# A hybrid attention and gMLP block on one core: small constants loaded at the end of the u stage, later weights of the vs stage issued behind the last token tile, squares tied two tiles behind the casts

## The chip, the cores and the metric

The kernel runs on one core of one Trainium2 chip. The time is device time in microseconds (us), from the start of one execution to its end. Three runs of the kernel before gave 931.64, 933.08 and 933.76 us, a median of 933.08. A profiled execution gives, beside its time, a trace of every instruction on every engine: TensorE (PE in the profile), its weight loads (PEld), VectorE (DVE), ScalarE (ACT), GpSimd (POOL) and SyncE (SP), which issues most of the data transfers (DMAs).

## The reference

One layer on 1024 tokens of width 1024, in float32:

```python
h = rmsnorm(x, norm_g)
q, k, v, za, u, vs, zs, gm = split(h @ w_in)
a   = window_sink_attention(rope(q), rope(k), v, att_sinks)   # 16 heads, one sink per head
a   = (a * silu(za)) @ w_att_out
vn  = layernorm(gelu(vs), sg_ln_g, sg_ln_b)
sgo = gelu(u) * (mask(sg_w) mixed over blocks of 128 tokens with vn, + sg_b)
sgo = (sgo * silu(zs)) @ w_sg_out
ga, gs = sigmoid(gm + b_merge)
out = rmsnorm(x + (ga * a + gs * sgo) @ w_o, final_g)
```

The change touches the parts that make `vs` and `u`, and the loads of five small inputs: `att_sinks` (16 numbers), `b_merge` (2048), `sg_ln_g` and `sg_ln_b` (1024 each), and the mixing weights `sg_w` (eight matrices of 128 x 128).

## The kernel before

**How a product is made.** Each float32 operand is split into a high part, which the matmul's number format holds exactly, and a low part, the rest (`split`, L155 on ACT and L156 on DVE). A product of two operands is then three matmuls: high by high, high by low, low by high. On top of this a projection of 1024 x 1024 by 1024 x 1024 is cut into 2 x 2 quarters, and these are multiplied by seven products instead of eight. The tokens' sums and differences for this are called forms: b11, b21, t1, t2, t3, b22, t4. The weights' sums are called s1 to s4; a11, a12, a21, a22 are the weights' quarters themselves.

**The vs stage (0 to about 106 us).** It is written out step by step, since the forms are made here for the first time. For each of eight token tiles (128 tokens by 1024) `load_x` issues a load into one of three buffers named wr (L487), `scale_of` squares and sums it on ACT (L536, the square is written to a throw-away buffer) and makes the reciprocal root, and `turned_half` scales half a tile on DVE (L544), transposes its four 128 x 128 blocks on PE (L548) and leaves them in a PSUM bank. `form_of` casts a form's high part on ACT (L559) and takes the low part on DVE (L560). Tiles 0 to 3 go through `first_tile`, tiles 4 to 7 through `second_tile`, which also adds quarters on POOL by DMAs that accumulate (`add_on`, L531). Between the tiles stand the products that are possible so far: `first_product` (a11 and a12), `by_s1`, `by_s4`. Then follow, each over the two halves of the weights, the late products t2 by s2, t3 by s3 and t4 by a22 (`late_product`).

**Which loads this stage needs.** Beside x: a11, a12, s1 at the start; s3, which is a21 loaded into the place of s1 (`load_part`, L612, two DMAs) and then increased by a11 with two accumulating DMAs; a22 (two DMAs into wr buffers); and the mixing weights mix_w (L778, into the buffer wT, whose earlier tenant is the throw-away buffer of the squares). A quarter of mix_w is set to zero by a memset on DVE (L779). The small constants are `sink_sb` (L841, two loads, each 64 partitions of four runs of 8 bytes), its negative `nsink_sb` (L844, one DVE operation), `bm_sb` (L845), `lg_sb` (L846) and `lb_sb` (L847), the last two 128 partitions of 32 bytes each. nsink and sinks are read in the attention stage, lg and lb in the mixing of the u stage, bm near the end of the program.

**The u stage (about 106 to 240 us)** makes u by `gemm_pair` for four pairs of column blocks. A pair has the products b11, t1, t2, b21, t3, b22, t4, in this order. The first, t2's, t3's and t4's share one PSUM accumulator; it is copied or added to x11, x12, x22 as it grows, in L359, L366 (ACT) and L376 (DVE: x22 −= accumulator). The t4 matmuls of a pair write that accumulator again, so they wait for L376. Between products `split_next` loads and splits the weights of later pairs (wr, L200, two rows of weights per pair, then L155, L156 and the sums L242), and `hook` runs the mixing of finished blocks (`mix`: matmuls L890, then L898 and L906 on DVE, and a store L457).

**What sets the order.** The program is written in one order, but a planner sets each engine's order from the dependences and its own costs. So in SP's order of the kernel before, the two sink loads, bm, lg, lb and the first bias load (L876) stand among the loads of x tiles 5 and 6, though they are written behind the t4 product. Three helpers bind the order: `after(second, first)` ties two instructions of one engine in order, without a semaphore; `paced(move)` makes a DMA's issue wait for the instruction last put into `pace[0]`, a product's last matmul or an ACT copy; and the buffers themselves. Every engine, and SP's and POOL's DMA issuing, runs its own instructions strictly in order.

Of the kernel before, what the change touches and what calls it, by code (L numbers as in the profile page):

```python
# [30 lines left out]
P = 128  # L31
# [21 lines left out]
def hybrid_tile(  # L53
# [16 lines left out]
    nc = tc.nc  # L70
# [12 lines left out]
    def bank(tag, dt=F32):  # L83
        return psum.tile([P, 512], dt, name=nm("ps_" + tag), tag="ps_" + tag, bufs=2)

    def mtile(shape, dt, tag, bufs, pool=None):
        return (pool or main).tile(shape, dt, name=nm(tag), tag=tag, bufs=bufs)
# [4 lines left out]
    def raw_tile():  # L92
        return mtile([P, D], F32, "wr", 3)
# [9 lines left out]
    ident = const.tile([P, P], F32, name="ident")  # L103
# [6 lines left out]
    sink_sb = const.tile([P, 8], F32, name="sink_sb")  # L110
    nsink_sb = const.tile([P, 8], F32, name="nsink_sb")
    bm_sb = const.tile([P, 16], F32, name="bm_sb")
    lg_sb = const.tile([P, KC], F32, name="lg_sb")
    lb_sb = const.tile([P, KC], F32, name="lb_sb")
# [15 lines left out]
    def rstd_of(ss, scale, base=EPS, n=1):  # L130

        ve = mtile([P, n], F32, f"st{n}", 16 if n == 1 else 5)
        nc.vector.tensor_scalar(ve[:], ss, scale, base, op0=ALU.mult, op1=ALU.add)
        rt = mtile([P, n], F32, f"st{n}", 16 if n == 1 else 5)
        nc.scalar.activation(rt[:], ve[:], AF.Sqrt)
        r0 = mtile([P, n], F32, f"st{n}", 16 if n == 1 else 5)
        nc.vector.reciprocal(r0[:], rt[:])
        e = mtile([P, n], F32, f"st{n}", 16 if n == 1 else 5)
        if n == 1:
            nc.vector.scalar_tensor_tensor(e[:], ve[:], r0[:], r0[:], op0=ALU.mult, op1=ALU.mult)  # L140
        else:
            nc.vector.tensor_mul(e[:], ve[:], r0[:])
            nc.vector.tensor_mul(e[:], e[:], r0[:])
        nc.vector.tensor_scalar(e[:], e[:], -0.5, 1.5, op0=ALU.mult, op1=ALU.add)
        nc.vector.tensor_mul(e[:], e[:], r0[:])
        return e
# [11 lines left out]
    def after(second, first):  # L158

        tc.add_manual_dep(  # L160
            second.ins,
            first.ins.name,
            mybir.DependencyInfo(mybir.DependencyClass.NoSync, mybir.DependencyReason.DATA),
            reason="order",
        )
# [5 lines left out]
    def slot(name, shape=(P, 4, HALF), dt=F32R):  # L171

        return mtile(list(shape), dt, "T_" + name, 1)
# [28 lines left out]
    def begin_job():  # L202
        n = len(begun)
        if n < written[0]:
            begun.append(n)
            units.extend(jobs[n]())
# [25 lines left out]
    def half_of(half):  # L232
        return slice(half * HALF, (half + 1) * HALF)
# [44 lines left out]
    pace = [None]  # L278

    def paced(move):  # L280

        if pace[0] is not None:
            tc.add_manual_dep(
                move.ins,
                pace[0].ins.name,
                mybir.DependencyInfo(mybir.DependencyClass.Sync, mybir.DependencyReason.DATA),
                reason="pace",
            )
# [159 lines left out]
    def part_of_early(every=2):  # L448
        hooks[0] += 1
        if early and hooks[0] % every == 0:  # L450
            early.pop(0)()
# [33 lines left out]
    def load_x(t):  # L485
        xt = raw_tile()
        nc.sync.dma_start(xt[:], x[t * P : (t + 1) * P, :])  # L487
        return xt
# [32 lines left out]
    def raw_sum(t):  # L521
        return x_place(0, 1, t)

    def raw_b21(t):
        return x_place(1, 0, t)

    g_of = list(g_in)
    casts, lows = [], []

    def add_on(dst, src):  # L530
        nc.gpsimd.dma_start(dst, src, accum_op=ALU.add)  # L531

    def scale_of(t):
        xt = x_in[t] if t in x_in else load_x(t)
        ss = mtile([P, 1], F32, "st1", 16)
        square = nc.scalar.activation(junk[:], xt[:], AF.Square, accum_out=ss[:])  # L536
        if t == 1:

            after(square, casts[-1])
        return xt, rstd_of(ss[:], 1.0 / D)  # L540

    def turned_half(xt, r, j):
        cs = half_of(j)
        nc.vector.scalar_tensor_tensor(xt[:, cs], xt[:, cs], r[:], g_of[j], op0=ALU.mult, op1=ALU.mult)  # L544
        pt = bank("sc")
        for i in range(4):
            k = j * 4 + i
            nc.tensor.transpose(pt[:, i * P : (i + 1) * P], xt[:, k * P : (k + 1) * P], ident[:])  # L548
        return pt

    def form_of(name, t, src, minus=False):
# [28 lines left out]
    def second_tile(t):  # L580
        xt, r = scale_of(t)
        if t == 4:
            hb.update(new_b(("t1", "b22")))
            f22.append(slot("t4l", dt=F32))
        pt = turned_half(xt, r, 0)
        nc.vector.tensor_sub(raw_sum(t), raw_sum(t), pt[:])
        nc.scalar.mul(nf12[t - 4][:], pt[:], -1.0)
        form_of("t1", t, by_k(raw_sum(t)))
        pt = turned_half(xt, r, 1)
        form_of("b22", t, by_k(pt[:]))  # L590
        nc.scalar.copy(f22[0][:, t - 4, :], pt[:])
        add_on(nf12[t - 4][:], f22[0][:, t - 4, :])

    def raw_t2(t):
        nc.vector.tensor_add(raw_sum(t), raw_sum(t), f22[0][:, t - 4, :])
        add_on(raw_b21(t), raw_sum(t))

    def w_vs(i, j, c):
        return w[W_VS + 4 * i + 2 * j + c]

    def two_k(v, c):
        return v[:, 2 * c : 2 * c + 2, :]

    def flat(v):
        return v.rearrange("p k n -> p (k n)")

    raws = {}

    def load_part(name, at, i, j):
        raws[name] = slot(at, dt=F32)  # L610
        for c in range(2):
            nc.sync.dma_start(flat(two_k(raws[name], c)), w_vs(i, j, c))  # L612

    def load_vs(c):
        nc.sync.dma_start(flat(two_k(raws["a11" if c < 2 else "a12"], c % 2)), w[W_VS + c])
# [10 lines left out]
    def split_w(name, c, src=None, behind=False):  # L626
        hi, lo = pair_of_w()
        (split_behind if behind else split)(hi[:], lo[:], flat(two_k(raws[name], c)) if src is None else src)
        keep_w(name, c, hi, lo)
# [20 lines left out]
    def vs_product(acc, name, t, weight, fresh, last=True, cs=(0, 1)):  # L650
        bh, bl = hb[name]
        for c in cs:
            for n in range(3):
                for k in (2 * c, 2 * c + 1):
                    wh, wl = vs_w[weight, k]
                    lt = (bh, bh, bl)[n][:, k, tokens(t)]
                    rt = (wh, wl, wh)[n]
                    mm = nc.tensor.matmul(
                        acc[:],
                        lt,  # L660
                        rt,
                        start=fresh and k == 0 and n == 0,
                        stop=k == 3 and n == 2,
                        skip_group_check=True,
                    )
        return mm
# [14 lines left out]
    def by_s1(t):  # L681
        t5s[t] = bank("o" if t < 2 else "sc")
        vs_product(t5s[t], "t1", t, "s1", True)
        nc.scalar.mul(x_place(1, 1, t), t5s[t][:], -1.0)

    def by_s4(t):
        vs_product(t5s[t], "b22", t, "s4", False)
# [10 lines left out]
    x_in[1] = load_x(1)  # L698
    split_vs(1)
    second = scale_of(1)  # L700
    for c in (2, 3):
        load_vs(c)
# [34 lines left out]
    raw_t2(4)  # L737
    by_s1(0)
    by_s1(1)
    load_part("s3", "t4h", 1, 0)  # L740
    for c in range(2):
        add_on(flat(two_k(raws["s3"], c)), w_vs(0, 0, c))
    second_tile(7)
    for t in range(4):
        to_x11(t)
    for t in (5, 6, 7):
        raw_t2(t)
    by_s4(0)
    by_s4(1)
    a22 = []  # L750
    for c in range(2):
        a22.append(raw_tile())
        nc.sync.dma_start(a22[c][:], w_vs(1, 1, c))
    by_s1(2)
    by_s1(3)
    split_w("s2", 0, behind=True)
# [18 lines left out]
                statistics(t + i, 0)  # L775

    mix_w = mtile([P, KC, P], F32, "wT", 1, pool)
    nc.sync.dma_start(mix_w[:], sg_w)  # L778
    nc.vector.memset(mix_w[64:128, :, 0:64], 0.0)  # L779
    ones = mtile([P, P], F32R, "ones", 1, pool)  # L780
    nc.vector.tensor_scalar(ones[:], ident[:], 0.0, 1.0, op0=ALU.mult, op1=ALU.add)
# [52 lines left out]
            nc.tensor.matmul(row_sums[half][:], ones[:], part[:, half_of(half)], start=n == 0, stop=n == 1)  # L834
    split_w("a22", 1, a22[1][:])
    part_of_early(1)
    begin_job()
    late_product("t4", "a22", to_x21, [split_next, lambda: gelu_of(4, 1), lambda: gelu_of(6, 1)])
    of_head = sinks.rearrange("(c e r) -> e c r", e=2, r=2)
    for e in range(2):  # L840
        nc.sync.dma_start(  # L841
            sink_sb[e * 64 : (e + 1) * 64].rearrange("p (c r) -> p c r", r=2), of_head[e].partition_broadcast(64)
        )
    after(nc.vector.tensor_scalar_mul(nsink_sb[:], sink_sb[:], -1.0), lows[-1])  # L844
    nc.sync.dma_start(bm_sb[:], b_merge)  # L845
    nc.sync.dma_start(lg_sb[:], ln_g)  # L846
    nc.sync.dma_start(lb_sb[:], ln_b)  # L847
    for _ in range(2):
        split_next()

# [3 lines left out]
    late = []  # L854
# [68 lines left out]
        gemm_pair(hb, finish, both)  # L923
    while late:
        late.pop(0)()
    stage.close()


# [768 lines left out]
    for p in range(4):  # L1697
        n, t, acc, x11 = N_PAIRS + p, T_ORDER[p], accs[p], firsts[p]
# [173 lines left out]
```

## Time and profile before

| | |
|---|---|
| three runs | 931.64, 933.08, 933.76 us |
| the profiled execution, its own time | 930.13 us |
| span of its trace | 928.4 us |
| instructions | 13190 |
| mean granted TensorE clock | 0.992 |
| busy PE, DVE, ACT, POOL | 898.3, 697.0, 526.9, 141.5 us |

How to read the rows that follow. A row of a timeline has the start in us, the duration in us, the engine, the line of the kernel, the operation, what it writes <- what it reads, the shapes, how many equal instructions the row groups, and in brackets the idle time before it and the instruction that ended it. SPq is SP's queue, where a row is the issue of a DMA, not its transfer. A row of windows has the window, its length, busy time and count for PE, PEld, DVE, ACT and POOL, the granted clock of PE (1.00 is full speed), the mean busy share of the DMA engines and the GB/s moved. The landing of a load is not a row of its own; it is read from the instruction that waited for it.

### The profile page before, as it was taken

Reading aid. Unit: us, or ns where it says so; the run is one execution under the profiler, and the core shown is the slowest. Engines: PE = TensorE matmul, PEld = TensorE weight load, DVE = VectorE, ACT = ScalarE, POOL = GpSimd, SP = SyncE. Lnnn points to the kernel's source line nnn. Section 1 sums busy time; section 2 is a strip of 40 time slices with the busy share of each in tenths; the row PEclk is TensorE's granted clock in tenths of the full one; section 3 lists DMA queues with packets and bytes.
Section 4 is the critical chain, followed back from the end, with each engine's and each line's share of the span. In section 5 each row is a group of like instructions: output and inputs, shape, how many; then the busy total and the mean of one; then the engine's idle time right before and its main releaser. Section 6 shows DMA issues by size and latency. Waiting matters only on the chain.

```text
span 928.4 us, 13190 instructions
## 1 busy us (share of the span) xinstructions
PE 898.3 (97%) x4284; PEld 746.8 (80%) x4284; DVE 697.0 (75%) x1263; ACT 526.9 (57%) x1058; POOL 141.5 (15%) x204
## 2 busy tenths in 40 slices
PE   8879989999999999999999999999998999999996
PEld 6668868888888778888888888888886887888885
DVE  6768695666668667887878888747798589579986
ACT  7647433333454466786667677756575475458443
POOL 2121212223011001120111111101100110210012
PEclk9999989999999999999999999999999999999999
DMA  8894968895778776678787777989868755998632
GB/s 295 224 241 114 269 207 166 151 193 176 258 252 265 237 228 148 200 214 185 197 215 235 246 232 186 235 303 379 276 244 316 259 201 160 296 301 294 204 113 114
DMA packets 131598, 209.57 MB, mean 226 GB/s; under 512 B 12649, under 2 KB 61033, under 8 KB 131530
## 3 DMA queue, kind: packets, MB, share of 16 engines
q1 hardware_dynamic: 110072, 149.74, 48.0%
q0 software_dynamic: 21312, 58.73, 28.1%
q8 instruction: 34, 0.56, 0.2%
q14 instruction: 34, 0.28, 0.1%
q10 hardware_dynamic: 146, 0.27, 0.1%
HBM read 147.74 MB, written 86.11 MB: 252 GB/s over the span
## 4 chain that ended last, share of the span: by engine, by line
PE 74%; DMA 9%; DVE 9%; issue 4%; ACT 1%; POOL 1%; SPq 1%; DVEq 0%; POOLq 0%; ACTq 0%
PE ps_mm L341 35%; PE ps_o L341 25%; PE ps_sc L1202 3%; DMA wr<-in_w_dram 3%; DMA T_t4h<-in_w_dram 3%; PE ps_tp L341 3%; PE ps_o L1287 2%; PE ps_sc L341 2%; PE ps_tp L1246 2%; DMA T_t3h<-T_t4h 2%; DVE wl L156 2%; PE ps_tp L890 2%; DVE bq L185 1%; DMA sums<-in_w_dram 1%; DVE xh L868 1%
## 5 line engine op out<-in xcount | busy, mean ns | idle before, releaser
L155 ACT CAST wh<-s 128x1024 fp32r<-128x1024 f32 (+1 forms) x78 | 78.1, 1004 | 86.0 <-PE ps_mm L341 46.8
L156 DVE TENSOR_TENSOR wl<-wr,wh 128x1024 fp32r<-128x1024 f32 (+1 forms) x78 | 73.1, 940 | 43.6 <-ACT wh L155 43.1
L155 ACT CAST wh<-wr 128x1024 fp32r<-128x1024 f32 (+1 forms) x78 | 64.0, 824 | 60.3 <-PE ps_mm L341 31.7
L156 DVE TENSOR_TENSOR wl<-s,wh 128x1024 fp32r<-128x1024 f32 (+1 forms) x78 | 90.9, 1166 | 9.1 <-ACT wh L155 9.0
L341 PE MATMUL ps_o<-T_t1h,wh 128*128 128x512 f32 x148 | 58.8, 397 | 0.8 <-ACT wh L155 0.7
L341 PE MATMUL ps_o<-T_b22h,wh 128*128 128x512 f32 x148 | 58.2, 394 | 0.0
L341 PE MATMUL ps_o<-T_b22l,wh 128*128 128x512 f32 x148 | 57.9, 391 | 0.0
L341 PE MATMUL ps_o<-T_b22h,wl 128*128 128x512 f32 x148 | 57.8, 390 | 0.0
L341 PE MATMUL ps_o<-T_t1h,wl 128*128 128x512 f32 x148 | 57.7, 390 | 0.0
L341 PE MATMUL ps_o<-T_t1l,wh 128*128 128x512 f32 x148 | 57.6, 389 | 0.0
L341 PE MATMUL ps_mm<-T_b11h,wl 128*128 128x512 f32 x140 | 54.8, 392 | 2.9 <-DVE wl L156 2.9
L341 PE MATMUL ps_mm<-T_t3h,wh 128*128 128x512 f32 x140 | 55.5, 397 | 2.0 <-ACT x L366 2.0
L341 PE MATMUL ps_mm<-T_t4h,wh 128*128 128x512 f32 x140 | 55.2, 394 | 0.8 <-DVE x L376 0.7
L341 PE MATMUL ps_mm<-T_t3l,wh 128*128 128x512 f32 x140 | 55.3, 395 | 0.6 <-DVE T_t3l L156 0.6
L341 PE MATMUL ps_mm<-T_t3h,wl 128*128 128x512 f32 x140 | 55.4, 395 | 0.0
L341 PE MATMUL ps_mm<-T_b11h,wh 128*128 128x512 f32 x140 | 55.2, 395 | 0.0
L341 PE MATMUL ps_mm<-T_b11l,wh 128*128 128x512 f32 x140 | 54.8, 392 | 0.0
L341 PE MATMUL ps_mm<-T_t4h,wl 128*128 128x512 f32 x140 | 54.7, 391 | 0.0
L341 PE MATMUL ps_mm<-T_t2l,wh 128*128 128x512 f32 x140 | 54.6, 390 | 0.0
L1215 ACT ACTIVATE pr<-ps_sc,sm 128x192 f32<-128x192 f32 (+2 forms) x128 | 50.8, 408 | 6.7 <-DVE sm L1211 5.5
L341 PE MATMUL ps_mm<-T_t2h,wl 128*128 128x512 f32 x140 | 54.5, 390 | 0.0
L341 PE MATMUL ps_mm<-T_t4l,wh 128*128 128x512 f32 x140 | 54.5, 390 | 0.0
(384 smaller groups left out, 2404.1 us busy)
## 6 DMA issues: line engine op xcount, KB each, us to landing
wr<-in_w_dram SPq DMA_DIRECT2D x86, 256.0 KB
sums<-in_w_dram POOLq DMA_DIRECT2D x20, 512.0 KB, 7.9
s<-sums SPq DMA_DIRECT2D x20, 512.0 KB
q_hl<-qhl SPq DMA_DIRECT2D x16, 512.0 KB
q<-q_hl SPq DMA_DIRECT2D x64, 128.0 KB
y_dr<-x POOLq DMA_DIRECT2D x28, 256.0 KB, 6.5
wr<-in_w_dram SPq DMA_DIRECT2D x12, 512.0 KB
g<-in_w_dram POOLq DMA_DIRECT2D x12, 512.0 KB, 6.6
```

The lines of the kernel that those rows point to most:

```text
L155: nc.scalar.copy(hi, src)
L156: return nc.vector.tensor_sub(lo, src, hi.bitcast(F32))
L185: op(dst[:, i : i + 2, :], a[:, i : i + 2, :], c[:, i : i + 2, :])
L341: nc.tensor.matmul(acc, lt, rt, start=fresh and k == 0 and n == 0, stop=k == 3 and n == 2, skip_group_check=True,)
L868: nc.vector.tensor_scalar(xh[:, t, :], xh[:, t, :], mv[:, t, 0:1], r[:, t : t + 1], op0=ALU.subtract, op1=ALU.mult)
L890: nc.tensor.matmul(pm[:, t * P : (t + 1) * P], xh[:, half * 4 + t, g * P : (g + 1) * P], bias[-1][1][:, g % 4, :], start=True, stop=True,)
L1202: nc.tensor.matmul(sc[:, i, k0:], q_of[:, c, i * P : (i + 1) * P], kt[:, f, k0:], start=f == 0, stop=f == 1,)
L1215: nc.scalar.activation(held_in[c, i], sc[:, i, lo:hi], AF.Exp, bias=nmax[:, c, i : i + 1], scale=-1.0, accum_out=sums[:, c, i : i + 1],)
L1246: nc.tensor.transpose(dst, pr[:, i, block * P : block * P + width], ident[:])
L1287: nc.tensor.matmul(po[:, cs], lt, rt, start=n == 0, stop=n == len(terms) - 1)
```

## The change

Five things are edited. The loads of s3, of a22 and of mix_w get a dependence on the last transpose emitted so far, which is that of tile 7 (`behind(move, turns[-1])`). The load of s3 and its two accumulating additions are written behind tile 7 and the additions of t2 instead of ahead of tile 7. `lg_sb` and `lb_sb` are loaded ahead of the t4 product and paced on the last t3 product matmul. The sink loads, nsink and bm are written behind the four pairs of u and paced on the instruction that is then in `pace[0]`, an ACT copy of pair 3. The squares of tiles 3 to 7 get an order behind a cast two tiles earlier.

The planner then gives these orders. On ACT nothing changes place. On PE the transposes of tile 7 stand one product matmul earlier. On DVE the memset of mix_w (with the small operation behind it) moves from ahead of tile 7's scaling to behind the low parts of the t2 form, and nsink moves from the t4 product to pair 3 of u, behind a mixing product (L906) and directly ahead of L376. On POOL the additions to s3 stand behind tile 7's own addition. On SP the sink loads, bm, lg and lb are gone from among the x loads; s3, a22 and mix_w follow each other behind the last x load; lg and lb stand behind the second weight row of pair 0 and ahead of the weights of pair 1; the first sink load stands ahead of the eight weight loads of pair 5, the second and bm between the first four and the last four of these.

```diff
+    def behind(move, first):
+        tc.add_manual_dep(
+            move.ins,
+            first.ins.name,
+            mybir.DependencyInfo(mybir.DependencyClass.Sync, mybir.DependencyReason.DATA),
+            reason="pace",
+        )
...
-        if t == 1:
-
-            after(square, casts[-1])
+        if t == 1 or t > 2:
+
+            after(square, casts[-1] if t == 1 else casts[2 * t - 3])
...
-            nc.tensor.transpose(pt[:, i * P : (i + 1) * P], xt[:, k * P : (k + 1) * P], ident[:])
+            turns.append(nc.tensor.transpose(pt[:, i * P : (i + 1) * P], xt[:, k * P : (k + 1) * P], ident[:]))
...
-    def load_part(name, at, i, j):
+    def load_part(name, at, i, j, late=False):
         raws[name] = slot(at, dt=F32)
         for c in range(2):
-            nc.sync.dma_start(flat(two_k(raws[name], c)), w_vs(i, j, c))
+            move = nc.sync.dma_start(flat(two_k(raws[name], c)), w_vs(i, j, c))
+            if late:
+                behind(move, turns[-1])
...
-    load_part("s3", "t4h", 1, 0)
-    for c in range(2):
-        add_on(flat(two_k(raws["s3"], c)), w_vs(0, 0, c))
     second_tile(7)
     for t in range(4):
         to_x11(t)
     for t in (5, 6, 7):
         raw_t2(t)
+    load_part("s3", "t4h", 1, 0, True)
+    for c in range(2):
+        add_on(flat(two_k(raws["s3"], c)), w_vs(0, 0, c))
...
-        nc.sync.dma_start(a22[c][:], w_vs(1, 1, c))
+        behind(nc.sync.dma_start(a22[c][:], w_vs(1, 1, c)), turns[-1])
...
-    nc.sync.dma_start(mix_w[:], sg_w)
+    behind(nc.sync.dma_start(mix_w[:], sg_w), turns[-1])
     nc.vector.memset(mix_w[64:128, :, 0:64], 0.0)
...
     part_of_early(1)
+    paced(nc.sync.dma_start(lg_sb[:], ln_g))
+    paced(nc.sync.dma_start(lb_sb[:], ln_b))
     begin_job()
     late_product("t4", "a22", to_x21, [split_next, lambda: gelu_of(4, 1), lambda: gelu_of(6, 1)])
-    of_head = sinks.rearrange("(c e r) -> e c r", e=2, r=2)
-    for e in range(2):
-        nc.sync.dma_start(
-            sink_sb[e * 64 : (e + 1) * 64].rearrange("p (c r) -> p c r", r=2), of_head[e].partition_broadcast(64)
-        )
-    after(nc.vector.tensor_scalar_mul(nsink_sb[:], sink_sb[:], -1.0), lows[-1])
-    nc.sync.dma_start(bm_sb[:], b_merge)
-    nc.sync.dma_start(lg_sb[:], ln_g)
-    nc.sync.dma_start(lb_sb[:], ln_b)
...
     while late:
         late.pop(0)()
+    of_head = sinks.rearrange("(c e r) -> e c r", e=2, r=2)
+    for e in range(2):
+        paced(
+            nc.sync.dma_start(
+                sink_sb[e * 64 : (e + 1) * 64].rearrange("p (c r) -> p c r", r=2),
+                of_head[e].partition_broadcast(64),
+            )
+        )
+    nc.vector.tensor_scalar_mul(nsink_sb[:], sink_sb[:], -1.0)
+    paced(nc.sync.dma_start(bm_sb[:], b_merge))
     stage.close()
```

More of the change, by code (lines that the diff above doesn't have):

```diff
@@ L527, in hybrid_tile @@
     g_of = list(g_in)
-    casts, lows = [], []
+    casts, lows, turns = [], [], []
     def add_on(dst, src):
         nc.gpsimd.dma_start(dst, src, accum_op=ALU.add)
+    def behind(move, first):
[5 more added lines that the diff above has]
+        )
     def scale_of(t):
```

## The prediction

> **What bounds the kernel now.** I read the page's head, the chain of work that ended last, and then the first stages window by window, because the change touches only the `vs` stage (to about 106 us) and the `u` stage behind it.
>
> ```profile
> span 928.4 us, 13190 instructions
> PE 898.3 (97%) x4284; PEld 746.8 (80%) x4284; DVE 697.0 (75%) x1263; ACT 526.9 (57%) x1058; POOL 141.5 (15%) x204
> PE 74%; DMA 9%; DVE 9%; issue 4%; ACT 1%; POOL 1%; SPq 1%; DVEq 0%; POOLq 0%; ACTq 0%
> ```
>
> TensorE (PE) is busy for 898 of 928 us, so a gain must come out of the 30 us in which it stands, or out of its clock. The windows say where these are. The columns are the window and its length, then busy time (and count) of PE, PEld, DVE, ACT and POOL, then the granted clock, the DMA share and GB/s.
>
> ```profile
> 20.00:58.00 38.00, 30.57 (x151) 24.00 (x149) 24.53 (x54) 23.18 (x45) 9.53 (x11) 1.00 0.94 240
> 58.00:64.00 6.00, 4.07 (x14) 2.99 (x15) 4.73 (x10) 2.32 (x5) 0.86 (x1) 0.72 1.12 231
> 64.00:106.00 42.00, 42.00 (x187) 34.75 (x186) 34.44 (x54) 26.50 (x36) 9.56 (x14) 1.00 0.62 157
> 106.00:140.00 34.00, 30.04 (x133) 24.68 (x132) 26.06 (x49) 12.21 (x18) 5.06 (x9) 0.90 0.72 238
> 140.00:204.00 64.00, 64.00 (x326) 54.20 (x325) 38.21 (x56) 21.27 (x31) 17.40 (x21) 1.00 0.86 164
> ```
>
> The token tiles (20 to 58 us) keep the DMA engines 94% busy, and PE loses 7.4 us there and more behind it. From 64 to 106 and from 140 to 204 us PE has no gap: a wait put there costs in full.
>
> **The change part by part.** Times are on the clock of before, unless said otherwise.
>
> *A. Constants leave the x loads.* SyncE (SP) issues in order; the rows show it, ScalarE (ACT) and PE around tiles 4 and 5:
>
> ```profile
> 18.06 0.33 SPq L487 DMA_DIRECT2D wr<-in_x_dram  x1
> 18.43 1.43 SPq L841 DMA_DIRECT2D sink_sb<-in_sinks_dram  x2
> 22.45 0.35 SPq L487 DMA_DIRECT2D wr<-in_x_dram  x1
> 27.23 1.06 ACT L536 ACTIVATE wT<-wr 128x1024 f32<-128x1024 f32 x1 [1.70 <-DMA wr<-in_x_dram]
> 31.23 1.06 ACT L563 CAST T_t2h<-T_t4h 128x1024 fp32r<-128x1024 f32 x1
> 32.81 0.63 PE L548 MATMUL ps_sc<-ident,wr 128*128 128x128 f32 x4 [1.55 <-DVE wr L544]
> 35.99 1.06 ACT L536 ACTIVATE wT<-wr 128x1024 f32<-128x1024 f32 x1 [3.70 <-DMA wr<-in_x_dram]
> 41.41 0.63 PE L548 MATMUL ps_sc<-ident,wr 128*128 128x128 f32 x4 [2.93 <-ACT T_t4l L591]
> ```
>
> Tile 4 is issued at 18.06 and squared, as it lands, at 27.23: 9.2 us. Tile 5 is issued at 22.45, behind the two sink loads (many pieces of 8 bytes), and squared as it lands at 35.99: 13.5 us. I price the two sink loads at the difference, 4.3 us. Without them tile 5 lands at about 31.7, before ACT is through the cast of 31.23 (32.3). ACT's wait of 3.70 goes, and it covers PE's wait of 2.93: −2.9 (ends 0, if tile 5 is late for another reason, and −4.5, if tile 4's wait of 1.55 at 32.81 went too).
>
> *B. mix_w goes behind the last tile, its memset behind the t2 forms.* VectorE (DVE) runs in order:
>
> ```profile
> 49.36 0.33 SPq L778 DMA_DIRECT2D wT<-in_sg_w_dram  x1
> 57.36 0.48 DVE L779 MEMSET wT<- 64x512 f32 x1 [4.79 <-DMA wT<-in_sg_w_dram]
> 59.00 1.42 DVE L544 SCALAR_TENSOR_TENSOR wr<-wr,st,xh 128x512 f32<-128x512 f32 x2
> 59.85 1.80 PE L548 MATMUL ps_sc<-ident,wr 128*128 128x128 f32 x8 [4.64 <-issue]
> ```
>
> Before tile 7's scaling (59.00) DVE has a memset that waits 4.79 us for mix_w. Tile 7 itself is not late. With the memset behind the four low parts of t2 the scaling starts near 53.7 and PE's 4.64 goes. The window of 58 to 64 us, behind that stop, ran at a clock of 0.72: 6 x 0.28 = 1.7 us, which goes too. Tile 7's transposes stand one product matmul earlier in PE's order, so I keep back 0.4 for a short wait. B is −5.9, A and B together −8.8 (ends −5.9, B alone, and −10.4).
>
> *C. s3, a22 and mix_w as one burst.* These five loads now wait on SP for tile 7's last transpose, the s3 additions on POOL stand behind tile 7's addition, and the memset is on DVE ahead of the t2 product's work.
>
> ```profile
> 76.92 1.05 ACT L155 CAST wh<-T_t4h 128x1024 fp32r<-128x1024 f32 x1
> 75.64 1.29 DVE L768 BATCH_NORM_STATS2 bn<-xh 128x6 f32<-128x512 f32 x2 [2.87 <-ACT xh L772]
> 85.24 0.61 PE L658 MATMUL ps_mm<-wh,T_t3h 128*128 128x512 f32 x2
> ```
>
> Five loads of 512 KB and two additions of 512 KB, 3.5 MB, take 14.6 us at the 240 GB/s of the tile window: 53 to 67.6. The s3 cast comes at 76.92 − 8.8 = 68.1, its first matmul at 76.4, so PE has 8 us in hand. DVE reaches the memset near 64, mix_w is the last of the five, and DVE has idle time (2.87 at 75.64) to make part of it good: +0.5 (ends 0, +3).
>
> *D. lg and lb (256 pieces of 32 bytes)* go behind pair 0's weights and ahead of pair 1's, on whose arrival DVE already waits:
>
> ```profile
> 116.02 0.69 DVE L242 TENSOR_TENSOR s<-wr 128x512 f32<-128x512 f32 x1 [6.11 <-DMA wr<-in_w_dram]
> ```
>
> They have half as many pieces as the two sink loads (512 pieces, 4.3): at most 4.3, at least 0, and I take +1.5, since by count it is 2 and some weights wait for buffers anyway.
>
> *E. The negated sinks.* nsink, a 0.17 us operation that waits for both sink loads, moves from the t4 product to pair 3 of `u`, just ahead of x22 −= acc (L376):
>
> ```profile
> 94.58 0.17 DVE L844 TENSOR_SCALAR nsink_sb<-sink_sb 128x8 f32<-128x8 f32 x1
> 193.00 0.58 ACT L366 COPY x<-ps_mm 128x512 f32<-128x512 f32 x1
> 194.40 8.97 SPq L200 DMA_DIRECT2D wr<-in_w_dram  x7
> 198.68 0.87 SPq L200 DMA_DIRECT2D wr<-in_w_dram  x1
> 198.27 0.69 DVE L906 TENSOR_TENSOR x<-x,ps_tp 128x512 f32<-128x512 f32 x1
> 199.10 0.69 DVE L376 TENSOR_TENSOR x<-x,ps_mm 128x512 f32<-128x512 f32 x1
> 199.82 0.63 ACT L918 ACTIVATE x<-x 128x512 f32<-128x512 f32 x1 [3.04 <-DVE x L376]
> 203.38 0.48 PE L341 MATMUL ps_mm<-T_t4h,wh 128*128 128x512 f32 x1
> 206.00:208.00 2.00, 2.00 (x14) 1.80 (x13) 0.00 (x0) 1.54 (x2) 0.00 (x0) 1.00 1.10 311
> 208.00:210.00 2.00, 2.00 (x11) 1.62 (x10) 0.00 (x0) 0.00 (x0) 0.00 (x0) 1.00 0.64 222
> 211.21 0.69 DVE L242 TENSOR_TENSOR s<-wr 128x512 f32<-128x512 f32 x1 [5.64 <-DMA wr<-in_w_dram]
> ```
>
> The sink loads are paced on ACT's copy of 193.00. In SP's order the first stands ahead of pair 5's eight weight loads (194.40 onward), the second behind four of them, where the fifth is issued now (198.68). The last of the eight lands at 211.2, when DVE's wait ends. Four loads of 128 KB, 512 KB, take 1.7 to 2.4 us at 311 to 222 GB/s, so the fourth lands near 209. With 0.5 for the first sink load ahead of it and 2.1 (half of 4.3) for the second, nsink can run at 211.6, and with its own 0.17 and 0.69 of L376 the accumulator is free at 212.5. PE's first t4 matmul writes the accumulator that L376 reads, and stands now at 203.38 without a wait: +9.1. Queued behind nsink on DVE are L376 and the sums and low parts of the next weights; ACT's gelu of x22 (199.82) waits too. DVE's wait of 5.64 for weights disappears under it.
>
> The ends: mix_w's load, issued at 49.36 and awaited till 57.36, took 8.0 us; 198.6 + 8.0 gives 206.6, with the same 0.9 behind it a stop of 4.1. Tile 5's 13.5 us gives 212.1 and 9.6; with lg and lb's late weights on top I allow 12. A stop starts a slow clock period:
>
> ```profile
> 120.97 0.50 PE L341 MATMUL ps_mm<-T_t3h,wh 128*128 128x512 f32 x1 [1.99 <-ACT x L366]
> 135.13 3.28 PE L890 MATMUL ps_tp<-wT,xh 128*128 128x128 f32 x16 [1.86 <-DVE x L906]
> ```
>
> Two stops of 1.9 us stand in the 106 to 140 us window, whose clock of 0.90 loses 3.4 us: 1.7 for each, and so +1.7 here. E is +10.8.
>
> *F. Squares two tiles behind the casts.* The order of ACT's instructions comes out the same as before; only the dependence is written down: 0.
>
> The sum: −8.8 + 0.5 + 1.5 + 10.8 = +4.0. The profiled execution has a span of 928.4 in a time of 930.1; it becomes 934.1. The median of the three runs, 933.1, stands 2.9 above the profiled time, so I predict 937.0.
>
> **The rivals.**
> *R1, the other side: the second sink load is early.* If it lands by 202.5, nsink and L376 are done when PE reaches 203.38, and E costs nothing: −6.8, 926.3. Up to a landing at 207.6 (stop 5.1 plus 1.7 = 6.8) the change still gains. For it: SP issues the load at about 198.6, 4 us before. Against it: tile 5's 13.5 us and tile 4's 9.2, and weights landing till 211.2. The Trainium skill, page "DMA: Bandwidth & Descriptors", section "Anatomy of one DMA — SWDGE (gpsimd) path", gives a transfer a fixed cost of about 2.0 us plus its bytes over 436 GB/s; by that a sink load of 2 KB would land at about 200.7 (an estimate from the page), PE would not stop, and the time would be R1's. The trace disagrees where it can be seen (13.5 us for 512 KB of x behind two sink loads, not 3.2), and the page fitted another queue than SP's.
> *R2: the memset stalls in its new place.* mix_w is now the last of five loads; if the burst takes 17 us or more, the memset holds the t2 stage's DVE work for the +3 of C: 940.
> *R3: tile 5 stays late.* The tile window's DMA share is 0.94 and the bytes of x, weights and additions are the same; if they and not the sink pieces hold tile 5, A's 2.9 is missing: 940.
>
> **How the numbers follow.** The forecast has 0.56, R1 0.16, R3 0.12, R2 0.11, the rest 0.05. The forecast's own range is 932 (a stop of 4.1) to 942 (a stop of 12, C at its end). The range reaches to R1 below and past R2 and R3 above: 926 to 943. A measurement of this kernel can tell about 0.2%, 1.9 us. Faster: R1 and a part of the forecast with a landing before 206, 0.20; within 0.2%: landings of 206 to 209, 0.12; slower 0.68.
>
> **What the profile after would show.** A: no wait of PE at tile 5, ACT's 3.70 gone. B: no wait before the memset ahead of tile 7, PE's 4.64 and the clock of 0.72 gone. C: mix_w's memset after the t2 low parts, with a wait under 1. D: the 6.11 at 116.02 about 1.5 longer. E: a DVE wait of some 12 us for the sink load in pair 3, a PE wait of about 9 ending on DVE's x, and a slow clock behind it. The prediction is wrong if the sink load lands before 207.6, which shows as a PE wait under 5.1 there, or if stages behind 64 us give back what A and B win, which shows as new waits for weights.

## The result and the profile after

The changed kernel takes 937.09 us (median of five runs, 936.37 to 938.56). The kernel before, run beside it, takes 931.68. The ratio is 1.0052, with a 95% interval of 1.0037 to 1.0068: the change makes the kernel 0.5% slower. The forecast was 937.0.

The head of the page of the changed kernel, and windows of it (columns as before: window, length, PE, PEld, DVE, ACT, POOL, clock, DMA share, GB/s):

```profile
span 935.3 us, 13186 instructions
PE 903.3 (97%) x4284; PEld 749.5 (80%) x4284; DVE 697.5 (75%) x1263; ACT 526.4 (56%) x1058; POOL 141.1 (15%) x204
...
50.00:58.00 8.00, 7.94 (x38) 6.12 (x38) 7.26 (x12) 3.62 (x6) 2.71 (x4) 1.00 0.85 209
58.00:64.00 6.00, 6.00 (x28) 4.95 (x28) 2.79 (x5) 4.83 (x9) 2.19 (x3) 1.00 1.03 296
64.00:82.00 18.00, 15.24 (x65) 11.73 (x64) 11.31 (x17) 10.37 (x14) 3.54 (x5) 1.00 0.88 217
198.70:202.10 3.40, 0.00 (x0) 0.00 (x0) 0.00 (x0) 0.00 (x0) 0.00 (x0) 1.00 1.08 220
202.10:208.93 6.83, 4.04 (x10) 3.18 (x11) 4.79 (x8) 2.20 (x3) 0.00 (x0) 0.50 0.39 129
```

The tile stage has become full: PE has no gap left from 50 to 64 us, where it stood 4.64 us and then ran at a clock of 0.72. A new hole stands behind it (64 to 82 us, 2.8 us empty), and a large one at 198 us, followed by 6.83 us at half clock.

Where time went is read by setting the same matmul of both traces side by side. First one row of the kernel before, the first matmul of the t2 product, then the timeline of the changed kernel:

```profile
74.36 0.61 PE L658 MATMUL ps_mm<-wh,T_t2h 128*128 128x512 f32 x2
```

```profile
50.95 1.27 PE L556 MATMUL ps_sc<-ident,wr 128*128 128x128 f32 x8
64.40 0.61 PE L668 MATMUL ps_mm<-wh,T_t2h 128*128 128x512 f32 x2
77.96 0.70 PE L668 MATMUL ps_mm<-wh,T_t3h 128*128 128x512 f32 x2 [1.68 <-DVE xh L805]
115.47 0.50 PE L341 MATMUL ps_mm<-T_t3h,wh 128*128 128x512 f32 x1 [2.85 <-ACT x L366]
204.04 0.17 DVE L937 TENSOR_SCALAR nsink_sb<-sink_sb 128x8 f32<-128x8 f32 x1 [10.57 <-DMA sink_sb<-in_sinks_dram]
204.88 0.79 PE L341 MATMUL ps_mm<-T_t4h,wh 128*128 128x512 f32 x1 [6.75 <-DVE x L376]
```

Against the rows of before that the prediction quotes (59.85, 85.24, 120.97, 203.38) and the 74.36 above:

| matmul | before | after | shift | part |
|---|---|---|---|---|
| tile 7's transposes | 59.85 | 50.95 | −8.90 | A and B |
| first of t2 | 74.36 | 64.40 | −9.96 | A and B with the clock |
| first of t3 | 85.24 | 77.96 | −7.28 | C takes back 2.7 |
| pair 1, t3 | 120.97 | 115.47 | −5.50 | C and D take back 1.8 more |
| pair 3, t4 | 203.38 | 204.88 | +1.50 | E costs 7.0 |
| end of the span | 928.4 | 935.3 | +6.9 | slow clock, 5.4 |

So ten microseconds are won in the first 64 and nearly seventeen given back. The last 5.4 are no waits: 1.8 of them are the half clock from 202.10 on (6.83 us at 0.50, of which PE stood still for the first 2.8), the other 3.6 are two half clock periods at 338 and 714 us, which are told at the end.

### The profile page after: what moved, and what is told of

Read it like the earlier page. It is cut to its first block, busy times and chain, and to the rows that moved or that the text cites. A ratio compares the mean times of both kernels' runs of the same rounds, so it can differ in the third digit from the quotient of the medians.

```text
span 935.3 us, 13186 instructions
## 1 busy us (share of the span) xinstructions
PE 903.3 (97%) x4284; PEld 749.5 (80%) x4284; DVE 697.5 (75%) x1263; ACT 526.4 (56%) x1058; POOL 141.1 (15%) x204
## 4 chain that ended last, share of the span: by engine, by line
PE 76%; DVE 10%; DMA 8%; issue 3%; ACT 2%; SPq 1%; DVEq 0%; POOL 0%; ACTq 0%; POOLq 0%
PE ps_mm L341 34%; PE ps_o L341 24%; DMA wr<-in_w_dram 4%; PE ps_sc L1215 3%; PE ps_tp L341 3%; PE ps_o L1300 2%; PE ps_sc L341 2%; PE ps_tp L1259 2%; DVE wl L156 2%; PE ps_o L668 2%; DMA xh<-xh 1%; DMA sink_sb<-in_sinks_dram 1%; DVE bq L185 1%; PE ps_sc L556 1%; PE ps_mm L668 1%
## 5 line engine op out<-in xcount | busy, mean ns | idle before, releaser
L341 PE MATMUL ps_mm<-T_t2h,wh 128*128 128x512 f32 x140 | 55.0, 393 | 0.0
```

The lines of the kernel that those rows point to most:

```text
L341: nc.tensor.matmul(acc, lt, rt, start=fresh and k == 0 and n == 0, stop=k == 3 and n == 2, skip_group_check=True,)
```

## The experiments

Each kernel ran beside the kernel before on the same chip; that one's medians were 930.9 to 931.1 us. The ratios stand with their 95% intervals. A gain over the changed kernel is given as the difference of two medians; where the ratios say another size, it stands beside it.

### nsink behind the kv pair

```diff
-    nc.vector.tensor_scalar_mul(nsink_sb[:], sink_sb[:], -1.0)
...
     gemm_pair(hb, finish, hook)
+    after(nc.vector.tensor_scalar_mul(nsink_sb[:], sink_sb[:], -1.0), term[0])
     stage.close()
```

> The changed kernel with one edit: nsink stands on DVE behind the last addition of the kv pair instead of ahead of L376 of pair 3; the loads stay where they are. Theory (nsink's wait for the second sink load holds DVE, L376 and so the accumulator): DVE's wait of 10.57 us at nsink, PE's wait of 6.7 us at the first t4 matmul and the slow clock period behind it (about 2 us) are gone, 937.1 - 8.7 = 928.4 us. Rival (the sink loads' small pieces cost by delaying pair 5's weights): a wait of like size comes back at the next weights, 935 to 937 us.

Measured: 924.22 us (921.32 to 932.06), ratio 0.9949 (0.9925 to 0.9973). The rows of its trace:

```profile
195.89 0.48 PE L341 MATMUL ps_mm<-T_t4h,wh 128*128 128x512 f32 x1
217.39 0.17 DVE L981 TENSOR_SCALAR nsink_sb<-sink_sb 128x8 f32<-128x8 f32 x1
```

The t4 matmul starts 9.0 us earlier than in the changed kernel and without a wait, though the loads stand where they stood. PE has no like wait behind it: DVE waits 6.25 us for the next weights (5.64 in the kernel before), and PE does not stop for it. So it is the place of nsink on DVE that costs, not the loads. The median fell by 12.9 us instead of 8.7, by the ratios 9.6. The profiled run has no half clock at all between 13 and 900 us, which the expectation did not count on; of the 9.0 us above, 6.75 are the stop and some 1.5 the half clock at 130.5 us that the changed kernel's trace has and this one lacks.

### Both sink loads ahead of the weights

```diff
     def begin_job():
         n = len(begun)
+        if n == 5:
+            load_sinks()
...
```

`load_sinks` holds the same two paced loads, which go from their place behind the pairs.

> The changed kernel with one edit: both sink loads stand ahead of all eight weight loads of pair 5 on SP, instead of one ahead and one between the fourth and fifth; nsink is ahead of L376 as it was (one operation earlier). Theory (the second load is late because it stands behind four weight loads in the queue, which landed at about 201): it lands near 196, L376 is done before 198, PE does not stop, 928.4 us. Rival (such a load takes some 10 us from its issue wherever it stands): it lands near 200, PE still stops for 2 to 4 us and a slow period follows, 932 to 935 us.

Measured: 933.71 us (926.22 to 940.53), ratio 1.0015 (0.9995 to 1.0036). In the trace (lines are 12 higher here):

```profile
185.50 1.33 SPq L206 DMA_DIRECT2D sink_sb<-in_sinks_dram  x2
196.98 0.17 DVE L941 TENSOR_SCALAR nsink_sb<-sink_sb 128x8 f32<-128x8 f32 x1 [7.24 <-DMA sink_sb<-in_sinks_dram]
197.91 2.04 PE L905 MATMUL ps_tp<-wT,xh 128*128 128x128 f32 x8 [3.62 <-DVE x L921]
```

The theory falls. With no weight load of pair 5 ahead of them the two loads still took 11.5 us from issue to use (185.50 to 196.98); in the changed kernel the second took 10.5 (193.49, below, to 204.04). The use at 196.98 lies near the theory's 196, but this trace stands 2.8 us earlier at the loads (185.50 against 188.26); counted from the issue, the time is the rival's. PE still stopped for 3.62 us, now at a mixing product, whose L921 stands behind nsink. The order behind four weight loads was a part of the delay only, and the DMA packets that the traces record say which part. In the changed kernel the second load's first piece starts at 199.59, 6.1 us behind its issue (6.1 to 7.2 in the seven traces with this order), and its 256 pieces take 3.9 us. With both loads ahead the first piece starts 1.9 us behind the issue, but all 512 pieces must then pass, which takes 8.6 us.

```profile
193.49 0.62 SPq L932 DMA_DIRECT2D sink_sb<-in_sinks_dram  x1
```

### One sink load of 64-byte runs

```diff
-    of_head = sinks.rearrange("(c e r) -> e c r", e=2, r=2)
+    paced(nc.sync.dma_start(heads_sb[:], sinks.partition_broadcast(P)))
+    of_head = heads_sb[:].rearrange("p (c e r) -> p e c r", e=2, r=2)
     for e in range(2):
-        paced(
-            nc.sync.dma_start(
-                sink_sb[e * 64 : (e + 1) * 64].rearrange("p (c r) -> p c r", r=2),
-                of_head[e].partition_broadcast(64),
-            )
-        )
+        at = slice(e * 64, (e + 1) * 64)
+        nc.vector.tensor_copy(sink_sb[at].rearrange("p (c r) -> p c r", r=2), of_head[at, e])
```

> The changed kernel with one edit: the sinks are loaded by one load of 128 runs of 64 bytes, ahead of pair 5's eight weight loads, and two small copies on DVE pick each partition's eight values, in place of two loads of 256 runs of 8 bytes. Theory (the number of pieces makes the load slow: 512 pieces took 11.5 us from issue with both loads ahead of the weights): a quarter of the pieces, landing 3 to 5 us behind the issue, no wait of DVE above 2 us there, no PE stop, 926 to 928 us. Rival (a small load waits some 10 us in the queue, whatever its pieces): DVE waits 5 us or more, PE stops by 3 to 4 us, 932 to 934 us.

Measured: 927.54 us (921.11 to 934.36), ratio 0.9966 (0.9938 to 0.9993).

```profile
185.84 0.38 SPq L930 DMA_DIRECT2D heads_sb<-in_sinks_dram  x1
192.86 0.35 DVE L934 COPY sink_sb<-heads_sb 64x8 f32<-64x8 f32 x2 [5.29 <-DMA heads_sb<-in_sinks_dram]
```

From the same place in the queue, and at the same time in the kernel, 128 pieces of 64 bytes took 7.0 us where 512 pieces of 8 bytes took 11.5. So 4.5 us go with the pieces, close to the 4.3 that the prediction read off tiles 4 and 5. The other 7.0 us belong to neither theory: the load was expected in 3 to 5, and DVE's wait of 5.29 is the rival's. By the packets of the trace the first piece starts 2.0 us behind the issue and the last 3.8 us later, 1.2 us before the use. What spreads 128 pieces over 3.8 us stays open. The median came out as the theory had it, since PE did not stop at the t4 matmul.

### The memset later

```diff
-    nc.vector.memset(mix_w[64:128, :, 0:64], 0.0)
...
+    after(nc.vector.memset(mix_w[64:128, :, 0:64], 0.0), added[-1])
     row_sums = [bank("sc") for half in range(2)]
```

`added[-1]` is the last x12 addition of t2.

> The changed kernel with one edit: the memset of mix_w stands on DVE behind the last x12 addition of the t2 product, just ahead of the split of mix_w, instead of behind the low parts of t2. Theory M (the memset's wait of 5.21 us for mix_w makes DVE late for the t3 product): PE's waits of 0.52, 1.68 and 0.56 us at 71 to 81 us go, 937.1 - 3.5 = 933.6 us. Theory Q (ACT is late, since its copy at 72.03 waits 5.44 us for POOL's last addition to b21, which stands behind the additions to s3): only the 0.52 goes, 936.5 us.

In the changed kernel the two candidates stand side by side, a DVE wait for mix_w and an ACT wait for an addition that POOL issues:

```profile
57.57 0.86 POOL L531 DMA_DIRECT2D T_t4h<-in_w_dram  x1 [2.09 <-DMA T_t4h<-in_w_dram]
59.23 0.86 POOL L531 DMA_DIRECT2D T_t4h<-in_w_dram  x1 [0.80 <-DMA T_t4h<-in_w_dram]
59.77 1.22 POOL L531 DMA_DIRECT2D xh<-xh  x1
68.02 0.48 DVE L789 MEMSET wT<- 64x512 f32 x1 [5.21 <-DMA wT<-in_sg_w_dram]
72.03 0.59 ACT L700 COPY xh<-ps_sc 128x512 f32<-128x512 f32 x1 [5.44 <-DMA xh<-xh]
73.59 1.23 DVE L156 TENSOR_TENSOR wl<-T_t4h,wh 128x1024 fp32r<-128x1024 f32 x1 [2.66 <-ACT wh L155]
77.13 0.68 DVE L805 TENSOR_TENSOR xh<-xh,ps_mm 128x512 f32<-128x512 f32 x1
```

With the memset later, measured: 936.02 us, ratio 1.0066 (1.0050 to 1.0083).

```profile
77.07 0.59 ACT L700 COPY xh<-ps_sc 128x512 f32<-128x512 f32 x1 [5.86 <-DMA xh<-xh]
83.01 0.70 PE L668 MATMUL ps_mm<-wh,T_t3h 128*128 128x512 f32 x2 [2.95 <-DVE xh L806]
87.15 0.48 DVE L831 MEMSET wT<- 64x512 f32 x1 [0.16 <-issue]
```

The memset no longer waits, and PE's stop at the t3 product is still there, now 2.95 us. The wait of 5.21 us on DVE, the larger-looking of the two by its place, was hidden. (The profiled run was 5 us later here for a stop of PE in the tile stage, 4.2 us at 41.6, where ACT waited for an addition on POOL; this shifts the rows and not their order.) Theory M falls.

### The additions to s3 behind the last addition to b21

```diff
...
-        add_on(flat(two_k(raws["s3"], c)), w_vs(0, 0, c))
+        after(add_on(flat(two_k(raws["s3"], c)), w_vs(0, 0, c)), t2_adds[-1])
```

> The changed kernel with one edit: on POOL the two additions to s3 stand behind the last addition to b21 (tile 7's) instead of ahead of it. Theory Q: ACT's wait of 5.44 us at 72.03 shrinks by several us, PE's waits of 1.68 and 0.56 us at 78 to 81 us go, 937.1 - 2.7 = 934.4 us. Theory M: nothing changes, 937 us.

Measured: 930.48 us, ratio 0.9997 (0.9985 to 1.0010).

```profile
57.12 0.86 POOL L531 DMA_DIRECT2D xh<-xh  x1 [1.97 <-DMA T_t4h<-in_w_dram]
57.66 1.21 POOL L531 DMA_DIRECT2D T_t4h<-in_w_dram  x1
...
75.03 0.62 PE L670 MATMUL ps_mm<-wh,T_t3h 128*128 128x512 f32 x2
```

The t3 product starts 2.93 us earlier (77.96 to 75.03) and with no wait. Theory Q holds: the last addition to b21 had got behind two 512 KB additions on POOL's queue, ACT's copy of a result into the place that this addition reads had to wait for it, the cast of s3 stood behind that copy on ACT, and the x12 additions behind the split on DVE. The gain of 6.6 us in the median (5.1 by the ratios) is more than the 2.7 expected; at pair 3 the shift of the trace is 5.3.

### Both edits

> The changed kernel with two edits: nsink behind the kv pair's last addition on DVE, and on POOL the additions to s3 behind the last addition to b21. Theory (the two costs stand in different stages and add): 924.2 - 4.3 = 919.9 us, with none of PE's waits at 78 to 81 us and no stop at the first t4 matmul of pair 3. Rival (the 4 us won by 81 us are lost again at pair 1's weights, for which DVE waits 6 us): the wait at 110 us grows by as much, 923 to 924 us.

Measured: 920.92 us (919.01 to 923.42), ratio 0.9899 (0.9874 to 0.9923). This is the fastest kernel here with the next one, 1.0% faster than the kernel before.

```profile
span 919.2 us, 13183 instructions
...
76.36 0.61 PE L670 MATMUL ps_mm<-wh,T_t3h 128*128 128x512 f32 x2
193.86 0.48 PE L341 MATMUL ps_mm<-T_t4h,wh 128*128 128x512 f32 x1
```

Neither matmul waits, and the t4 matmul of pair 3 stands at 193.86 against 203.38 before: 9.5 of the early ten microseconds arrive.

### lg and lb earlier

The kernel with both edits, and lg and lb behind mix_w:

```diff
+    behind(nc.sync.dma_start(lg_sb[:], ln_g), turns[-1])
+    behind(nc.sync.dma_start(lb_sb[:], ln_b), turns[-1])
...
-    paced(nc.sync.dma_start(lg_sb[:], ln_g))
-    paced(nc.sync.dma_start(lb_sb[:], ln_b))
```

> The kernel of the run before (nsink late, the additions to s3 behind) with one edit: lg and lb are loaded right behind mix_w, ahead of pair 0's second weights, instead of ahead of pair 1's weights. Theory D (their 256 pieces delay pair 1's weights by about 1 us): DVE's wait of 6 us for them shrinks by 1 to 1.5 us and 920.9 becomes 919.9 us. Rival (pair 1's weights are late for their own bytes): no change, 920.9 us.

Measured: 920.95 us, ratio 0.9892 (0.9873 to 0.9911): no difference that these runs can tell, but the 1 us expected lies within the interval of 1.8 us to either side, so theory D is neither shown nor excluded. DVE's wait for pair 1's weights, 5.48 us, did not shrink below what the kernels with lg and lb late show in single runs (4.10 in the kernel with both edits). In its profiled run the t3 product of pair 1 starts 1.5 us before that of the kernel with both edits (111.47), and this is lost again to one half clock period more:

```profile
105.04 0.69 DVE L242 TENSOR_TENSOR s<-wr 128x512 f32<-128x512 f32 x1 [5.48 <-DMA wr<-in_w_dram]
110.00 0.50 PE L341 MATMUL ps_mm<-T_t3h,wh 128*128 128x512 f32 x1 [0.54 <-ACT x L366]
```

### The sinks back among the x loads

The sink loads and nsink are written where the kernel before has them; all else is as in the changed kernel.

> The changed kernel with one edit: the two sink loads and nsink are written where they were before, and come out between the loads of tiles 4 and 5 and in the t4 product. Theory A (the sink loads' pieces make tile 5 late): ACT's wait before tile 5's square and a PE wait of about 2.9 us at tile 5 come back, and the cost of nsink in pair 3 is gone: 924.2 + 3.4 = 927.6 us. Rival R3 (tile 5 was late for the bytes of the tile window): PE does not stop at tile 5, 924.2 us as with nsink late.

Measured: 930.15 us, ratio 0.9988 (0.9968 to 1.0009), 5.9 us over the kernel with nsink late (3.6 by the ratios; 3.4 were expected). Its rows:

```profile
40.40 1.06 ACT L544 ACTIVATE wT<-wr 128x1024 f32<-128x1024 f32 x1 [4.80 <-DMA wr<-in_x_dram]
42.08 1.12 PE L556 MATMUL ps_sc<-ident,wr 128*128 128x128 f32 x4 [3.40 <-ACT T_t4l L599]
```

PE's stop comes back, 3.40 us with a slow clock behind it, on an x load that is late. It is tile 6 here and tile 5 before. Theory A holds in kind, R3 does not: the bytes loaded for the tiles are the changed kernel's, whose squares of tiles 5 and 6 do not wait:

```profile
31.66 1.08 ACT L544 ACTIVATE wT<-wr 128x1024 f32<-128x1024 f32 x1
...
35.89 1.06 ACT L544 ACTIVATE wT<-wr 128x1024 f32<-128x1024 f32 x1
```

The DMA engines say why. In the kernel before the 512 pieces pass from 24.7 to 31.4 us, by the packets of its trace. A window within this time (DMA share and GB/s at the end), first of the kernel before, then of the changed one:

```profile
25.00:29.00 4.00, 4.00 (x23) 3.38 (x22) 1.16 (x4) 2.30 (x6) 0.85 (x1) 1.00 0.17 44
```

```profile
25.00:29.00 4.00, 4.00 (x23) 3.38 (x22) 2.58 (x8) 3.23 (x8) 0.85 (x1) 1.00 1.06 283
```

With the sinks there, the engines are busy for 0.17 to 0.48 of this window in three traces (the kernel before, this one and the memset alone); without them for 0.79 to 1.06 in the nine others. Before the squares of tiles 4 to 6 ACT waits 4.8 to 6.0 us for x in those three traces and at most 2.1 in the nine. So the x loads are late while the engines have room, and not for the bytes.

### The memset alone

The kernel before, with the memset behind the low parts of t2 and no load moved:

```diff
+    last_low = lows[-1]
...
-    nc.vector.memset(mix_w[64:128, :, 0:64], 0.0)
+    after(nc.vector.memset(mix_w[64:128, :, 0:64], 0.0), last_low)
```

> The kernel before with one edit: the memset of mix_w stands on DVE behind the low parts of t2 instead of ahead of tile 7's scaling; no load is moved. Theory B (the memset's wait of 4.79 us holds tile 7's scaling, PE's stop of 4.64 us and the slow clock behind it follow): 931.0 - 5.9 = 925.1 us, and the memset has no wait, as mix_w has landed at 57. Rival (tile 7 is late for another reason): PE still stops there, 930 to 931 us.

Measured: 925.07 us (922.75 to 931.19), ratio 0.9944 (0.9922 to 0.9967).

```profile
58.38 1.41 DVE L544 SCALAR_TENSOR_TENSOR wr<-wr,st,xh 128x512 f32<-128x512 f32 x2
60.97 1.03 PE L548 MATMUL ps_sc<-ident,wr 128*128 128x128 f32 x8
72.76 0.48 DVE L780 MEMSET wT<- 64x512 f32 x1 [0.16 <-issue]
```

PE's 4.64 us at tile 7 are gone and the memset waits for nothing. One line moved on one engine is worth 5.8 us (5.2 by the ratio), close to the predicted 5.9. (The profiled run itself has other stops in the tile stage and a span of 928.8; the median is the measure here.)

### Without the order of the squares

```diff
-        if t == 1 or t > 2:
-            after(square, casts[-1] if t == 1 else casts[2 * t - 3])
+        if t == 1:
+            after(square, casts[-1])
```

> The changed kernel without the order of the squares behind the casts; the order of instructions is the same on every engine. Theory F (the pin costs and brings nothing): the time of the changed kernel, 937.1 us within 1.5. Rival (the pin sets a wait that matters): another time by more than 2 us.

Measured: 934.92 us, ratio 1.0041 (1.0023 to 1.0060), against 1.0052 (1.0037 to 1.0068) for the changed kernel: the intervals overlap. The median lies 0.7 us outside the expected band. Since the order of instructions is the same, this is taken as what a repetition differs by, about 2 us.

## Why the prediction was right, and where it was not

The time was met, and the reason named for it, nsink's wait, is shown by the first experiment. The terms were met less well:

| step | predicted | measured |
|---|---|---|
| A and B, tile stage | −8.8 | −9.96 (64.40 against 74.36); B alone −5.8 in its own run |
| C, the burst | +0.5 | about +3.5 (−9.96 at t2, −6.5 three matmul rows into t3, 81.48 against 87.96) |
| D, lg and lb | +1.5 | at most 1.0 in the trace, not to be told from 0 in its own run |
| E, nsink | +10.8 | 7.0 + 1.8 = +8.8 in the trace |
| F, squares | 0 | 0 within the repetition |
| sum | +4.0 | +3.3 to 209 us |

*A and B* came out by the mechanism named: the square of tile 5 does not wait, the scaling of tile 7 is not held. *C* is the step that failed. It weighed the burst by its bytes against the s3 cast and the memset (seven times 512 KB at 240 GB/s are 15.3 us, not 14.6; 15.7 were measured), and named the additions to s3 "behind tile 7's addition" on POOL; it did not follow what they pass on that queue. Tile 7's last addition to b21 was now behind them, and ACT's copy at 72.03 paid for it. The memset's stall, R2's, came (5.21 us, where a wait under 1 was forecast), though the burst was shorter than the 17 us that R2 asks for: it began at 52.29, and mix_w was used at 68.02. It cost nothing that the runs show: moving it brought no gain. *D* was over-sized. *E* was right in its place and 2 us too large, and two of its parts were off in opposite directions. On the clock of before, 5.5 us later than that of the changed kernel, the second load's pieces began at 205.1 and ended at 209.0. The prediction has the weights ahead of them in the way until 209, 4 us too long, and gives these pieces 2.1 us where they took 3.9.

The prediction's sign of being wrong, that stages behind 64 us give back what A and B win, came in part: 3.5 of the ten microseconds went back by 82 us, by a wait for an addition on POOL and not by new waits for weights.

R1 did not come: nsink ran at 204.04, which with the shift of −5.5 is 209.5 on the clock of before, past the break-even of 207.6. The rule of the Trainium skill, page "DMA: Bandwidth & Descriptors", section "Anatomy of one DMA — SWDGE (gpsimd) path", that a transfer costs about 2.0 us plus its bytes over 436 GB/s, would have put it at about 200.7; 7.0 to 11.5 us from issue to use were measured here, on SP's queue and not on the GpSimd path that the page fits.

Last, the step from the profiled run to the median. The prediction added 2.9 us, since the profiled run of before lay that far under the median of three. More runs put that median at 930.9 to 931.7, 0.8 to 1.6 above the profiled time, and the changed kernel's profiled run is its median. With that the sum of +4.0 would have given about 935. In the two traces the steps up to 209 us came to +3.3, and the half clock periods at 338 and 714 us, which no step of the prediction had, added 3.6. The 2.9 added for the median stood, by chance, in the place of these. That the number fell on the measured one to 0.1 us is luck: the terms (A and B together, C, D and E) were off by 0.5 to 3 us, and not all the same way.

## What to carry to other kernels

An operation that waits for a load is priced by what stands behind it on its in-order engine, not by its own 0.17 us: place it behind the last operation that TensorE needs soon, as the stop of 6.75 us behind nsink and the 5.8 us of one memset show. A load of many small pieces is priced by its pieces and by the queue ahead of it, not by its 2 KB. When a DMA with accumulation is moved on a queue, list every entry that it now stands ahead of and who waits for each; the 3.5 us of C came from the one that was not listed. Of two long waits that stand side by side, take away one at a time: the one of 5.21 us on DVE was hidden, the one of 5.44 us on ACT was paid in part, with PE stops of 1.68 and 0.56 us.

## What the runs showed that was not expected

The half clock does not follow from a stop's length alone. The same stop of 1.75 us, of the same matmul, in the kernel before (first fence) and in the changed one (second), with windows of 3.41 us laid as the half clock periods of each trace repeat:

```profile
707.92 0.50 PE L341 MATMUL ps_mm<-T_b11h,wl 128*128 128x512 f32 x1 [1.75 <-DVE wl L156]
...
705.71:709.13 3.42, 1.67 (x7) 1.06 (x7) 3.42 (x6) 0.30 (x1) 0.37 (x1) 1.00 1.04 389
709.13:712.54 3.41, 3.41 (x16) 2.81 (x16) 3.41 (x5) 0.43 (x1) 1.25 (x3) 1.00 1.04 392
```

```profile
713.27 0.50 PE L341 MATMUL ps_mm<-T_b11h,wl 128*128 128x512 f32 x1 [1.75 <-DVE wl L156]
...
710.67:714.08 3.41, 1.54 (x6) 0.98 (x7) 3.41 (x5) 0.69 (x2) 0.00 (x0) 1.00 1.03 381
714.08:717.49 3.41, 3.41 (x10) 2.64 (x9) 3.41 (x6) 0.00 (x0) 1.62 (x3) 0.51 1.05 399
```

In the first window PE works 1.67 of 3.42 us and the next window runs at full clock; in the second it works 1.54 of 3.41 and the next runs at 0.51. Within each of the traces the half clock periods begin at whole multiples of 3.41 us from each other (in the changed kernel 130.5, 202.1, 338.7 and 714.1: 21, 40 and 110 steps), with another offset in each execution. In the traces of this case, windows of that grid at full clock with PE idle for 54% and more were followed by a half clock window with one exception, those idle for 46% and less were not, with one exception the other way, and those between went both ways. A stop of some 1.7 us, half a window, so costs 1.7 us more or nothing, by where it falls, and this fits the spread of several us between runs of one kernel. It was read off the traces, and no run was made to test it alone. The Trainium skill, page "TensorE: Matmul & The Clock Gate", section "HAM oscillation — how this bites in real kernels", warns of idle gaps above about 3.4 us; here stops of 1.75 and 1.85 us (ending at 713.27 and 129.63) were enough. It also means that an edit can seem to gain more than its stop is long, when the stops that remain fall under half a window: between the two profiled runs nsink late gained 14.1 us (935.3 to 921.2) for a stop of 6.75.
